# Attention scores in a two-layer decoder: from plain fp32 products to split single-pass products over 128 rows

## The chip, the cores and the metric

The kernel runs on one core of a Trainium2 chip. The metric is the time of one execution on the device, in microseconds (us); for the kernel before it is the median of three runs. Five engines work beside each other, each with its own queue in strict order: TensorE (PE in the profile, its weight loads PEld), VectorE (DVE), ScalarE (ACT), GpSimd (POOL) and SyncE (SP), which here issues DMAs. An instruction starts when those ahead of it on its engine have gone and when the semaphores that it waits for allow.

## The reference

256 tokens, 2048 features, two layers. The first is a retention layer, the second multi-head latent attention (MLA) with 16 heads; a squared-ReLU MLP follows each. All is fp32. The change touches the scores of the second layer: each head has a part of 128 features without position (`nope`) and a rotary part of 64 (`pe`), and the keys' rotary part is the same for all heads.

```python
q = (c_q @ w_uq).reshape(b, s, H, MLA_NOPE_DIM + MLA_ROPE_DIM)
q_nope = rms_norm(q[..., :MLA_NOPE_DIM], q_nope_norm)
q_pe = apply_rope(rms_norm(q[..., MLA_NOPE_DIM:], q_pe_norm), cos[:, :, None], sin[:, :, None])
...
sc = jnp.einsum('bhqd,bkhd->bhqk', qn, k_nope) + jnp.einsum('bhqr,bkr->bhqk', qp, k_pe)
sc = sc.astype(jnp.float32) * scale
sc = jnp.where(kpos[None, :] <= qpos[:, None], sc, -jnp.inf)
p = jax.nn.softmax(sc, axis=-1).astype(v.dtype)
return jnp.einsum('bhqk,bkhd->bqhd', p, v)
```

## The kernel before

**Split products.** A large product is made of parts: a matrix is split into `h`, rounded to a type with a short mantissa that PE takes in one pass (fp32r), and `l`, what is left. `split` (L131 to L137) writes `h` on ACT and `l` on DVE. PE then adds up three products, h by h, h by l and l by h (L192 to L194). Weights come by DMA into `raw` and are split half by half into `wh` and `wl`, each with five buffers. The small products of attention are plain fp32, which the profile counts as two passes each.

**Stages of the second layer.** Shared latent and rotary key (`kd`, `downed`), query latent (`dq`), keys and values (`ku`, `keyed`), queries and attention (`uq`), output projection (`wo`). Keys, queries and attention go in 8 blocks of two heads. The 256 tokens are two tiles of 128 (t = 0, 1).

**One block of attention.** `query` is called when the block's product is complete: ACT copies it from PSUM with its token scale (`qs`, L697). DVE squares it (`qu`), sums the squares of both parts, POOL makes the reciprocal roots (`qn_r`, `qp_r`), DVE multiplies by them (L705, L708) and rotates the `pe` part in four steps (L582 to L585). This is one norm chain for each token tile. Three pieces of weight product later PE transposes both parts (`qntp`, `qptp`), ACT copies them to SBUF (`qt`, `qpe`), and one piece later `score` (L739, L740) makes the products; a `pe` product has 64 rows, a `nope` product 128. DVE adds the mask (`p`, L745), takes maxima; ACT makes the exponentials; DVE divides. Two pieces later PE transposes `p` (`ptp`), ACT copies (`pt`), and `values` makes the products with the values (`ao`), which are split into `ot` for the output projection.

**What sets the order.** The code issues a block's steps some pieces of the weight product later (`later`, `tick`). A scheduler then orders each engine's queue by its own estimate of when operands and buffers are ready, so that an edit in one place moves rows of others. Tiles with one tag share a fixed number of buffers: `f2k` (14, among them `qs`, `qu`, `qt`, `qpe`, `p`, `pt`), `act` (20), PSUM `acc` (4), `tp` (2, for all transposes and for `ao`).

Of the kernel before, what the change touches and what calls it, by code (L numbers as in the profile page):

```python
# [49 lines left out]
def yoco(ctx: ExitStack, tc: tile.TileContext, a):  # L50
# [21 lines left out]
    def act_tile(name, dtype=F32R):  # L72
        """Two blocks of 128 features, each with its two halves (of precision, as a rule) side by side."""
        return pool.tile([P, 2, 2, S], dtype, tag="act", bufs=20, name=name)

    # Work that waits for other engines is issued some pieces of a product later.
    queue = []
# [18 lines left out]

# [1 line left out]
    gains = pool.tile([P, G_ALL], F32, name="gains")  # L98
# [15 lines left out]

# [1 line left out]
    def rstd(total, n, w, name):  # L116
        """(total / n + eps) ** -0.5 for [P, w] sums of squares."""
        m = small(w, f"{name}_m")
        nc.gpsimd.tensor_scalar(m, total, 1.0 / n, EPS, op0=ALU.mult, op1=ALU.add)
        r = small(w, f"{name}_r")  # L120
        nc.gpsimd.tensor_tensor(r, m, neg_half[:, :w], op=ALU.pow)
        return r
# [5 lines left out]
    def split(h, l, src, scale=None):  # L128
        """h + l = src * scale, each of 12 bits."""
        if scale is None:  # L130
            nc.scalar.copy(h, src)  # L131
            nc.vector.tensor_tensor(l, src, h.bitcast(F32), op=ALU.subtract)  # L132
        else:
            nc.scalar.activation(h, src, AF.Copy, scale=scale)  # L134
            nc.vector.scalar_tensor_tensor(
                l, src, scale, h.bitcast(F32), op0=ALU.mult, op1=ALU.subtract
            )  # L137
# [8 lines left out]
    def transposed(srcs, name):  # L146
        """[tokens, 128] pairs of both token tiles -> [128, 2, S] in PSUM."""
        tp = bank("tp", [2, S], name)
        for j in range(2):
            for t in range(NT):  # L150
                nc.tensor.transpose(tp[:, j, t * P : (t + 1) * P], srcs(t, j), ident)
        return tp

    def stream(w, chunk, cols, name, use, done=None, before=None):
        """use(half, parts of the weights) for both halves of a chunk of the weights."""
        raw = pool.tile([P, 2048], F32, tag="raw", bufs=3, name=f"{name}_raw")
        if before is None:
            nc.sync.dma_start(raw[:, :cols], w[chunk])
        n = cols // 2
        for half in range(2):  # L160
            wh = pool.tile([P, 1024], F32R, tag="wh", bufs=5, name=f"{name}_wh{half}")
            wl = pool.tile([P, 1024], F32R, tag="wl", bufs=5, name=f"{name}_wl{half}")
            cuts = 1
            if before is not None:
                cuts = 1 if half else 2
                m = n // cuts
                for i in range(cuts):
                    lo = half * n + i * m
                    nc.sync.dma_start(raw[:, lo : lo + m], w[chunk][:, lo : lo + m])
                    if i == 0:  # L170
                        before(half)
            m = n // cuts
            for i in range(cuts):
                lo = half * n + i * m
                split(wh[:, i * m : (i + 1) * m], wl[:, i * m : (i + 1) * m], raw[:, lo : lo + m])
# [132 lines left out]

# [81 lines left out]

# [33 lines left out]
    def ret_rope(acc, out, name, wait):  # L424
        """One head's rotated q or k by feature: [128, dk half, S]."""
        u = f2k([2, S], f"{name}_u")
# [110 lines left out]

# [1 line left out]
    def mlp(layer, act, row, done):  # L539
# [34 lines left out]

# [1 line left out]
    def pe_rope(dst, u, src, t, i, heads):  # L576
        """dst = the rotation of src [P, heads, ROPE], gains in the tables."""

# [10 lines left out]
    rc, ckv = [], []  # L589
    kpe_t = pool.tile([P, S], F32, name="kpe_t")  # L590

    def downed(acc, b):
# [8 lines left out]
        for t in range(NT):  # L601
# [9 lines left out]
            pe_rope(kp[:, 0, 0:1], kp[:, 1, 0:1], kp[:, 1, 1:2], t, 0, 1)  # L611
            nc.vector.tensor_copy(kp[:, 0, 1], kp[:, 0, 0])
            kps.append(kp)

        def turn():
            tp = bank("tp", [S], "kpe_tp")
            for t in range(NT):
                nc.tensor.transpose(tp[:, t * P : (t + 1) * P], kps[t][:, 0].rearrange("p h c -> p (h c)"), ident)
            nc.scalar.copy(kpe_t, tp)
# [10 lines left out]

# [1 line left out]
    ssq = [small(3, f"ssq{t}") for t in range(NT)]  # L632
# [25 lines left out]

# [1 line left out]
    k_t, v_s = [], []  # L660

    def keyed(acc, b):
        kv = act_tile(f"kv{b}", F32)
        kt, vt = kv[:, 0], kv[:, 1].rearrange("p t (h c) -> p t h c", h=2)
        v_s.append(vt)
# [13 lines left out]
        def turn():  # L679
            tp = transposed(lambda t, j: kr[t][:, 1, j], f"kntp{b}")  # L680
            nc.scalar.activation(kt, tp, AF.Copy, scale=gain(G_KN))
            k_t.append(kt)
# [5 lines left out]

# [1 line left out]
    nc.vector.tensor_scalar(gqn, gain(G_QN), scale, None, op0=ALU.mult)  # L690
    o_act = []

    def query(acc, b):
        qr = []
        for t in range(NT):
# [18 lines left out]
            pe_rope(pe.rearrange("p (h c) -> p h c", h=2), tmp, q[:, :, NOPE:], t, 1, 2)  # L714
            qr.append((q, pe))

        def turn():
            tp = transposed(lambda t, j: qr[t][0][:, j, 0:NOPE], f"qntp{b}")
            qt = f2k([2, S], f"qt{b}")
            nc.scalar.activation(qt, tp, AF.Copy, scale=gqn)  # L720
            tp = bank("tp", [S], f"qptp{b}")
            for t in range(NT):
                nc.tensor.transpose(tp[:, t * P : (t + 1) * P], qr[t][1], ident)
            qpe = f2k([S], f"qpe{b}")
            nc.scalar.copy(qpe, tp)
# [3 lines left out]

    def score(b, qt, qpe):  # L730
        """Scores [query, head, keys of tile 0 for both query tiles, then tile 1], then softmax."""
        sc = two_banks(f"s{b}")
        for hh in range(2):
            rows = slice(hh * ROPE, (hh + 1) * ROPE)
            for t in range(NT):
                dst = sc[:, hh, t * P : t * P + (t + 1) * P]
                qs = slice(t * P, (t + 1) * P)
                n = (t + 1) * P
                nc.tensor.matmul(dst, qt[:, hh, qs], k_t[b][:, hh, :n], start=True, stop=False)  # L739
                nc.tensor.matmul(dst, qpe[rows, qs], kpe_t[rows, :n], start=False, stop=True)  # L740
        p = [f2k([2, (t + 1) * P], f"p{b}{t}") for t in range(NT)]
# [138 lines left out]
```

## Time and profile before

| | us |
|---|---|
| Median of 3 runs (lowest, highest) | 2568.24 (2568.08, 2568.37) |
| Span of the profiled execution | 2566.0 |
| PE busy | 2554.7 |
| DVE busy | 1475.5 |
| ACT busy | 1233.7 |
| POOL busy | 135.7 |

The profiled execution's own time is not recorded apart from its span; the span is 2.2 us under the median. A row of a timeline gives the start in us from the span's start, the duration, engine, line, operation, output and inputs with shapes, a count of merged operations (x2) and, in brackets, the idle time of the engine before it and what ended it. Matmuls overlap, so the cost of one is the distance to the next start, not its duration.

### The profile page before, as it was taken

The page shows a single profiled execution, that of the slowest core. Times are in us where ns is not written, and L with a number is a line of the kernel's source. Part 1 is how long each engine was busy: PE and PEld are TensorE (multiplying, and loading weights), DVE is VectorE, ACT ScalarE, POOL GpSimd, SP SyncE. Part 2 cuts the span into 40 slices and gives each one's busy share as a digit, 9 for nine tenths or more (in the row PEclk, how much of TensorE's full clock was granted, in tenths as well). Part 3 has the DMA queues.
Part 4 walks back from the last instruction along what each step waited for, and adds up shares of the span by engine and source line. Part 5 has one row for each costly group of instructions (what it writes and reads, how often), then busy time and mean ns, then how long its engine had stood idle before and what let it go on. Part 6 is the DMA issues. An engine that isn't in the chain of part 4 may idle for free.

```text
span 2566.0 us, 31690 instructions
## 1 busy us (share of the span) xinstructions
PE 2554.7 (100%) x12786; PEld 2168.1 (84%) x12786; DVE 1475.5 (58%) x1828; ACT 1233.7 (48%) x1651; POOL 135.7 (5%) x211
## 2 busy tenths in 40 slices
PE   8999999999999999999999999999999999999999
PEld 7888888888888888888888888998888888888887
DVE  6655555554556644654565656776666446645654
ACT  6444444443445533543454566554555435534542
POOL 6200000000000000000000002221000000000000
PEclk9999999999999999999999999999999999999999
DMA  8555555555555555555555464444455555555554
GB/s 297 182 177 180 181 181 183 182 184 186 190 183 192 183 197 194 184 188 191 196 182 196 148 221 152 148 144 148 174 188 182 196 197 181 191 190 193 184 202 140
DMA packets 71571, 473.85 MB, mean 185 GB/s; under 512 B 8192, under 2 KB 9344, under 8 KB 18176
## 3 DMA queue, kind: packets, MB, share of 16 engines
q1 hardware_dynamic: 71280, 471.78, 52.1%
q8 instruction: 100, 1.64, 0.2%
q14 instruction: 47, 0.39, 0.0%
q10 hardware_dynamic: 144, 0.05, 0.0%
HBM read 469.70 MB, written 2.10 MB: 184 GB/s over the span
## 4 chain that ended last, share of the span: by engine, by line
PE 97%; POOL 2%; DMA 0%; DVE 0%; issue 0%; SPq 0%; DVEq 0%
PE u_acc L220 19%; PE u_acc L216 9%; PE d_acc L192 9%; PE d_acc L194 9%; PE d_acc L193 9%; PE ro_acc L194 2%; PE ro_acc L193 2%; PE ro_acc L192 2%; PE rv_acc L192 2%; PE rv_acc L194 2%; PE rv_acc L193 2%; PE rk_acc L220 2%; PE rq_acc L220 2%; PE rg_acc L192 2%; PE rg_acc L194 2%; PE rg_acc L193 2%
## 5 line engine op out<-in xcount | busy, mean ns | idle before, releaser
L220 PE MATMUL u_acc<-n,u_wh 128*128 128x512 f32 x2048 | 718.1, 398 | 0.0
L216 PE MATMUL u_acc<-n,u_wl 128*128 128x256 f32 x2048 | 564.8, 281 | 0.0
L132 DVE TENSOR_TENSOR d_wl<-d_raw,d_wh 128x1024 fp32r<-128x1024 f32 x256 | 313.6, 1225 | 321.6 <-ACT d_wh L131 321.6
L220 PEld LDWEIGHTS u_acc<-n,u_wh 128*128 128x128 f32 x2048 | 381.0, 188 | 88.8
L132 DVE TENSOR_TENSOR u_wl<-u_raw,u_wh 128x1024 fp32r<-128x1024 f32 x256 | 313.3, 1224 | 241.1 <-ACT u_wh L131 241.1
L131 ACT CAST d_wh<-d_raw 128x1024 fp32r<-128x1024 f32 x256 | 269.8, 1054 | 374.0 <-PE d_acc L194 347.4
L192 PE MATMUL d_acc<-d_wh,hid 128*128 128x512 f32 x1024 | 398.6, 389 | 0.0
L194 PE MATMUL d_acc<-d_wh,hid 128*128 128x512 f32 x1024 | 398.4, 389 | 0.0
L193 PE MATMUL d_acc<-d_wl,hid 128*128 128x512 f32 x1024 | 398.4, 389 | 0.0
L131 ACT CAST u_wh<-u_raw 128x1024 fp32r<-128x1024 f32 x256 | 269.1, 1051 | 260.2 <-PE u_acc L220 210.2
L216 PEld LDWEIGHTS u_acc<-n,u_wl 128*128 128x128 f32 x2048 | 386.7, 189 | 5.6
L194 PEld LDWEIGHTS d_acc<-d_wh,hid 128*128 128x128 f32 x1024 | 192.3, 188 | 40.0
L193 PEld LDWEIGHTS d_acc<-d_wl,hid 128*128 128x128 f32 x1024 | 192.3, 188 | 39.8
L192 PEld LDWEIGHTS d_acc<-d_wh,hid 128*128 128x128 f32 x1024 | 192.3, 188 | 39.4
L132 DVE TENSOR_TENSOR ro_wl<-ro_raw,ro_wh 128x1024 fp32r<-128x1024 f32 x64 | 78.4, 1225 | 84.2 <-ACT ro_wh L131 84.2
L132 DVE TENSOR_TENSOR rg_wl<-rg_raw,rg_wh 128x1024 fp32r<-128x1024 f32 (+1 forms) x68 | 78.9, 1166 | 60.9 <-ACT rg_wh L131 60.9
L131 ACT CAST ro_wh<-ro_raw 128x1024 fp32r<-128x1024 f32 x64 | 67.4, 1053 | 94.6 <-PE ro_acc L194 86.5
L192 PE MATMUL rg_acc<-rg_wh,a 128*128 128x512 f32 x256 | 101.1, 396 | 5.7 <-ACT a L134 5.7
L132 DVE TENSOR_TENSOR rv_wl<-rv_raw,rv_wh 128x1024 fp32r<-128x1024 f32 x64 | 79.3, 1250 | 41.3 <-ACT rv_wh L131 41.3
L131 ACT CAST rg_wh<-rg_raw 128x1024 fp32r<-128x1024 f32 (+1 forms) x68 | 67.8, 998 | 72.9 <-PE rv_acc L194 46.7
L193 PE MATMUL rg_acc<-rg_wl,a 128*128 128x512 f32 x256 | 100.3, 392 | 0.2 <-DVE rg_wl L132 0.2
L192 PE MATMUL rv_acc<-rv_wh,a 128*128 128x512 f32 x256 | 100.4, 392 | 0.0
(260 smaller groups left out, 4072.5 us busy)
## 6 DMA issues: line engine op xcount, KB each, us to landing
u_raw<-in_mlp_w SPq DMA_DIRECT2D x128, 1024.0 KB, 4.8
d_raw<-in_mlp_w SPq DMA_DIRECT2D x128, 1024.0 KB, 4.8
rv_raw<-in_ret_w_gv SPq DMA_DIRECT2D x32, 1024.0 KB, 4.7
ro_raw<-in_ret_w_out SPq DMA_DIRECT2D x32, 1024.0 KB, 4.7
rg_raw<-in_ret_w_gv SPq DMA_DIRECT2D x28, 1024.0 KB, 4.7
uq_raw<-in_mla_w_uq SPq DMA_DIRECT2D x24, 768.0 KB, 4.3
rq_raw<-in_ret_w_qk SPq DMA_DIRECT2D x16, 1024.0 KB, 4.8
rk_raw<-in_ret_w_qk SPq DMA_DIRECT2D x16, 1024.0 KB, 4.7
```

The lines of the kernel that those rows point to most:

```text
L131: nc.scalar.copy(h, src)
L132: nc.vector.tensor_tensor(l, src, h.bitcast(F32), op=ALU.subtract)
L192: nc.tensor.matmul(acc[t], ah, rh, start=k == 0, stop=False)
L193: nc.tensor.matmul(acc[t], ah, rl, start=False, stop=False)
L194: nc.tensor.matmul(acc[t], al, rh, start=False, stop=k == nk - 1)
L216: nc.tensor.matmul(acc[f][:, 0:S], wl[:, cols], a[:, 0], start=False, stop=False)
L220: nc.tensor.matmul(acc[f], wh[:, cols], a.rearrange("p i s -> p (i s)"), start=k == 0, stop=k == nk - 1)
```

## The change

Queries and keys of the scores are split into h and l, as weights are, and the score becomes five single-pass products for each head and token tile: three for the 128 `nope` features, and two for the rotary part. For these the 64 rotary features of a query's h and l are stacked to 128 rows (`qpp`, transposed into `qpe`). The rotary key is stored twice: once with its h in both halves, once with its l in the upper and zeros in the lower half (`parts` in `downed`), so that two products give (h + l) by h and h by l. `kt` and the values `v` become separate tiles of the `act` pool. `qt` is now two tiles, and for each token tile a `qpp` is added, all from `f2k`. Comments and docstrings were removed as well.

```diff
-    kpe_t = pool.tile([P, S], F32, name="kpe_t")
+    kpe_t = pool.tile([P, 2, S], F32R, name="kpe_t")
...
-            nc.vector.tensor_copy(kp[:, 0, 1], kp[:, 0, 0])
-            kps.append(kp)
+            parts = f2k([2, 2, ROPE], f"kpp{t}", F32R)
+            for i in range(2):
+                nc.scalar.copy(parts[:, 0, i], kp[:, 0, 0])
+            nc.vector.tensor_tensor(parts[:, 1, 0], kp[:, 0, 0], parts[:, 0, 0].bitcast(F32), op=ALU.subtract)
+            nc.vector.memset(parts[:, 1, 1].bitcast(F32), 0.0)
+            kps.append(parts.bitcast(F32))
...
-            for t in range(NT):
-                nc.tensor.transpose(tp[:, t * P : (t + 1) * P], kps[t][:, 0].rearrange("p h c -> p (h c)"), ident)
+            tp = transposed(lambda t, j: kps[t][:, j].rearrange("p h c -> p (h c)"), "kpe_tp")
...
-            nc.scalar.activation(kt, tp, AF.Copy, scale=gain(G_KN))
+            kt = act_tile(f"kt{b}")
+            split(kt[:, 0], kt[:, 1], tp, gain(G_KN))
...
-            qr.append((q, pe))
+            parts = f2k([2, 2, ROPE], f"qpp{b}{t}", F32R)
+            pe = pe.rearrange("p (h c) -> p h c", h=2)
+            split(parts[:, :, 0], parts[:, :, 1], pe)
+            qr.append((q, parts.bitcast(F32)))
...
-            qt = f2k([2, S], f"qt{b}")
-            nc.scalar.activation(qt, tp, AF.Copy, scale=gqn)
-            tp = bank("tp", [S], f"qptp{b}")
-            for t in range(NT):
-                nc.tensor.transpose(tp[:, t * P : (t + 1) * P], qr[t][1], ident)
-            qpe = f2k([S], f"qpe{b}")
+            qt = [f2k([2, S], f"qt{b}{i}", F32R) for i in range(2)]
+            split(qt[0], qt[1], tp, gqn)
+            tp = transposed(lambda t, j: qr[t][1][:, j].rearrange("p i c -> p (i c)"), f"qptp{b}")
+            qpe = f2k([2, S], f"qpe{b}", F32R)
             nc.scalar.copy(qpe, tp)
...
-                nc.tensor.matmul(dst, qt[:, hh, qs], k_t[b][:, hh, :n], start=True, stop=False)
-                nc.tensor.matmul(dst, qpe[rows, qs], kpe_t[rows, :n], start=False, stop=True)
+                qh, ql = (i[:, hh, qs] for i in qt)
+                kh, kl = (k_t[b][:, i, hh, :n] for i in range(2))
+                nc.tensor.matmul(dst, qh, kh, start=True, stop=False)
+                nc.tensor.matmul(dst, qh, kl, start=False, stop=False)
+                nc.tensor.matmul(dst, ql, kh, start=False, stop=False)
+
+                for i in range(2):
+                    nc.tensor.matmul(dst, qpe[:, hh, qs], kpe_t[:, i, :n], start=False, stop=i == 1)
```

The queues move with it. The first place is ACT between two scores, where the queries of block 4 are copied out of PSUM (`qs`, tile 0 and tile 1) and the transposed queries of block 3 to SBUF (`qt`, `qpe`). Lines are those of each kernel. Before:

```order
L131 CAST uq_wh_13690<-uq_raw 128x768
L697 ACTIVATE qs_13535<-uq_acc_13396,cq_r 128x384
L131 CAST uq_wh_13708<-uq_raw 128x768
L697 ACTIVATE qs_13556<-uq_acc_13397,cq_r 128x384
L720 ACTIVATE qt_13582<-qntp_13577,gqn 128x512
L725 COPY qpe_13587<-qptp_13584 128x256
L131 CAST uq_wh_13724<-uq_raw 128x768
L770 COPY pt_13593<-ptp_13589 128x384
```

In the changed kernel (`qpp_13650` and `qpp_13674` are the rotary parts of block 4, tile 0 and tile 1; `qs_13653` is its tile 1; its tile 0 was copied earlier, behind the `pt` of the score before):

```order
L131 CAST uq_wh_13952<-uq_raw 128x768
L131 CAST qpp_13650<-qu_13631 128x2x64
L701 ACTIVATE qs_13653<-uq_acc_13479,cq_r 128x384
L131 CAST uq_wh_14017<-uq_raw 128x768
L131 CAST uq_wh_14033<-uq_raw 128x768
L131 CAST qpp_13674<-qu_13655 128x2x64
L134 ACTIVATE qt_13682<-qntp_13677,gqn 128x512
L131 CAST uq_wh_14051<-uq_raw 128x768
L730 CAST qpe_13691<-qptp_13686 128x512
L780 COPY pt_13697<-ptp_13693 128x384
```

The second tile's `qs` has moved behind the first tile's `qpp`, and `qt` of block 3 behind the second tile's `qpp` of block 4.

The second place is DVE at the same point: the norm chains of the two tiles. Before:

```order
L705 TENSOR_TENSOR qs_13535<-qs_13535,qn_r 128x2x128
L708 TENSOR_TENSOR qs_13535<-qs_13535,qp_r 128x2x64
L699 TENSOR_TENSOR qu_13558<-qs_13556 128x384
L582 TENSOR_TENSOR qu_13537<-qs_13535,petab_82 128x128
L583 TENSOR_TENSOR qu_13537<-qs_13535,petab_82 128x2x32
L584 TENSOR_TENSOR qu_13537<-qs_13535,petab_82 128x2x32
L701 TENSOR_REDUCE sq_13560<-qu_13558 128x2
L585 TENSOR_TENSOR qu_13537<-qu_13537 128x128
L702 TENSOR_REDUCE sq_13560<-qu_13558 128x2
L705 TENSOR_TENSOR qs_13556<-qs_13556,qn_r 128x2x128
```

In the changed kernel, from the end of the first tile's chain:

```order
L585 TENSOR_TENSOR qu_13631<-qu_13631 128x128
L132 TENSOR_TENSOR uq_wl_13953<-uq_raw,uq_wh_13952 128x768
L132 TENSOR_TENSOR qpp_13650<-qu_13631,qpp_13650 128x2x64
L703 TENSOR_TENSOR qu_13655<-qs_13653 128x384
L705 TENSOR_REDUCE sq_13657<-qu_13655 128x2
L706 TENSOR_REDUCE sq_13657<-qu_13655 128x2
L132 TENSOR_TENSOR uq_wl_14018<-uq_raw,uq_wh_14017 128x768
L709 TENSOR_TENSOR qs_13653<-qs_13653,qn_r 128x2x128
...
L585 TENSOR_TENSOR qu_13655<-qu_13655 128x128
L132 TENSOR_TENSOR qpp_13674<-qu_13655,qpp_13674 128x2x64
L135 SCALAR_TENSOR_TENSOR qt_13683<-qntp_13677,gqn,qt_13682 128x512
```

The two chains were interleaved and now stand one after the other; behind them stands the low part of `qt`.

The third place is PE at the score of block 3. Before:

```order
L194 MATMUL uq_acc_13602<-uq_wh_13621,cq_11856 128x384
L739 MATMUL s_13637<-kv_12388,qt_13582 128x128
L740 MATMUL s_13637<-kpe_t,qpe_13587 128x128
L739 MATMUL s_13637<-kv_12388,qt_13582 128x256
L740 MATMUL s_13637<-kpe_t,qpe_13587 128x256
```

In the changed kernel:

```order
L745 MATMUL s_13741<-kt_12559,qt_13682 128x128
L746 MATMUL s_13741<-kt_12559,qt_13682 128x128
L192 MATMUL uq_acc_13932<-uq_wh_13936,cq_11856 128x384
L193 MATMUL uq_acc_13932<-uq_wl_13937,cq_11856 128x384
L778 MATMUL ptp_13693<-cst,p_13535 128x128
L778 MATMUL ptp_13693<-cst,p_13536 128x128 x2
L778 MATMUL ptp_13699<-cst,p_13535 128x128
L778 MATMUL ptp_13699<-cst,p_13536 128x128 x2
L747 MATMUL s_13741<-kt_12559,qt_13683 128x128
L750 MATMUL s_13741<-kpe_t,qpe_13691 128x128 x2
```

The score's first two products now stand before two of uq and the transposes of `p` of the block before, the other eighteen behind them.

More of the change, by code (lines that the diff above doesn't have):

```diff
@@ L611, in downed @@
             pe_rope(kp[:, 0, 0:1], kp[:, 1, 0:1], kp[:, 1, 1:2], t, 0, 1)
-            nc.vector.tensor_copy(kp[:, 0, 1], kp[:, 0, 0])
-            kps.append(kp)
+            parts = f2k([2, 2, ROPE], f"kpp{t}", F32R)
[4 more added lines that the diff above has]
+            kps.append(parts.bitcast(F32))
         def turn():
-            tp = bank("tp", [S], "kpe_tp")
-            for t in range(NT):
-                nc.tensor.transpose(tp[:, t * P : (t + 1) * P], kps[t][:, 0].rearrange("p h c -> p (h c)"), ident)
+            tp = transposed(lambda t, j: kps[t][:, j].rearrange("p h c -> p (h c)"), "kpe_tp")
             nc.scalar.copy(kpe_t, tp)
@@ L657, in yoco @@
         gemm(a["mla_w_dq"], b * 4, act_q, KD, 512, f"dq{b}", lambda acc, b=b: queried(acc, b))
-    k_t, v_s = [], []
+    k_t, v_s, vs = [], [], []
     def keyed(acc, b):
-        kv = act_tile(f"kv{b}", F32)
-        kt, vt = kv[:, 0], kv[:, 1].rearrange("p t (h c) -> p t h c", h=2)
+        if b % 2 == 0:
+            vs.append(act_tile(f"v{b}", F32))
+        vt = vs[-1][:, b % 2].rearrange("p t (h c) -> p t h c", h=2)
         v_s.append(vt)
@@ L733, in score @@
         for hh in range(2):
-            rows = slice(hh * ROPE, (hh + 1) * ROPE)
             for t in range(NT):
```

## The prediction

> **What bounds the kernel now.** I read the page first, then the waits of TensorE (PE), then timelines of the query stage, where the change lies. The first rows are from the page, the last from the waits of PE.
>
> ```profile
> span 2566.0 us, 31690 instructions
> PE 2554.7 (100%) x12786; PEld 2168.1 (84%) x12786; DVE 1475.5 (58%) x1828; ACT 1233.7 (48%) x1651; POOL 135.7 (5%) x211
> PE rg_acc L192 <- ACT a L134: 5.7, 1, 5.7
> ```
>
> PE is busy for the whole span but for 5.7 us at the start. What is taken from PE shortens the kernel, and any wait put into its queue lengthens it, one for one. The span stands to the median of the runs, 2568.24 us, as 2566.0 and 2.2 us around it; I carry the 2.2.
>
> One turn of the query stage, from score to score, in the table of stretches (columns: length, then busy time of PE, PEld, DVE, ACT, POOL):
>
> ```profile
> 1673.62:1692.95 19.33, 19.33 (x109) 17.35 (x109) 14.89 (x38) 9.97 (x21) 4.82 (x8) 1.00 0.38 130
> ```
>
> PE fills its 19.33 us. DVE is busy for 14.9 of them: little room before it, too, is a bound. PE's own rows of that turn, and two of the key stage for a price:
>
> ```profile
> 1687.43 0.60 PE L151 MATMUL qntp<-cst,qs 128*128 128x128 f32 x4
> 1687.87 0.38 PE L723 MATMUL qptp<-cst,qu 128*128 128x128 f32 x2
> ...
> 1692.96 0.38 PE L739 MATMUL s<-kv,qt 128*128 128x128 f32 x2
> 1693.28 0.48 PE L740 MATMUL s<-kpe_t,qpe 64*128 64x128 f32 x2
> 1693.69 0.70 PE L739 MATMUL s<-kv,qt 128*128 128x256 f32 x2
> ...
> 1697.04 0.70 PE L779 MATMUL ao<-pt,kv 128*128 128x256 f32 x2
> ...
> 1698.37 0.42 PE L192 MATMUL uq_acc<-uq_wh,cq 128*128 128x384 f32 x1
> 1698.62 0.34 PE L193 MATMUL uq_acc<-uq_wl,cq 128*128 128x384 f32 x1
> 1698.80 0.34 PE L194 MATMUL uq_acc<-uq_wh,cq 128*128 128x384 f32 x1
> ```
> ```profile
> 1484.10 0.28 PE L194 MATMUL kd_acc<-kd_wh,n 128*128 128x256 f32 x1
> 1484.22 0.28 PE L192 MATMUL kd_acc<-kd_wh,n 128*128 128x256 f32 x1
> ```
>
> Durations overlap, so prices are distances between starts. A score costs 1697.04 - 1692.96 = 4.08 us: each plain product is two passes (x2). A split product (fp32r) is one pass; at 256 columns they follow each other every 0.12 us. Transposes follow every 0.44 / 4 = 0.11 us, and a uq product takes 0.18 us.
>
> **What PE gains.** Per score, 8 plain products (4.08 us) become 20 single passes, ten of 256 columns and ten of 128. For 256 columns I take 0.12 us. A split product of 128 columns stands nowhere in this trace: its lower bound is the transposes' 0.11 us, its upper one the 0.41 us / 2 = 0.21 us of a pass in the row at 1693.28. I take 0.11, since it has the same shape as the transposes and one pass; hence 20 x 0.115 = 2.3 us. Eight scores save 8 x (4.08 - 2.3) = 14.2 us. Against it stand two more transposes per score and two for the rotary key, 18 x 0.11 = 2.0 us. Net, PE has 12.2 us less to do, and a turn would be 19.33 - 4.08 + 2.3 + 0.22 = 17.8 us if nothing made PE wait.
>
> **What the others gain, and where it lies.** The key splits add one DVE operation for each of 8 head pairs (0.6 us, by the `ot` row below, of the same size). In the new order each stands ahead of a multiply that waits for POOL:
>
> ```profile
> 1588.23 0.43 DVE L676 TENSOR_TENSOR kn<-kn,kn_r 128x256 f32<-128x256 f32 x1 [1.09 <-POOL kn_r L121]
> ```
>
> It fits into that 1.09 us, so I cost it at nothing; without that cover it is 8 x 0.6 = 4.8 us of DVE time, which the six weight splits in a row after the stage partly take up.
>
> The query splits are another matter, because of their place. The new order puts, on ACT, the copies of the rotary parts (`qpp`) of block b+1 ahead of `qt` of block b, and `qs` of the second token tile behind the first tile's `qpp`. Each `qpp` waits for DVE's whole norm and rotation of its tile. So PE's score b waits for `qt`, that for two norms one after the other, and these begin only after score b-1: a loop, which the old order does not have (there nothing on ACT ahead of `qt` waits for DVE). I go round it with prices from one turn of the old trace, on DVE, ACT and POOL:
>
> ```profile
> 1680.32 1.01 DVE L745 TENSOR_TENSOR p<-s,cst 128x256 f32<-128x256 f32 x2
> 1681.76 0.40 ACT L755 ACTIVATE p<-p,mx 128x128 f32<-128x128 f32 x1 [1.86 <-DVE mx L750]
> 1682.17 0.68 DVE L132 TENSOR_TENSOR ot<-ao,ot 128x512 fp32r<-128x512 f32 x1
> 1683.53 1.56 ACT L131 CAST uq_wh<-uq_raw 128x768 fp32r<-128x768 f32 x2
> 1683.87 1.01 DVE L761 TENSOR_SCALAR p<-p,inv 128x128 f32<-128x128 f32 x4
> 1684.79 2.69 DVE L132 TENSOR_TENSOR uq_wl<-uq_raw,uq_wh 128x768 fp32r<-128x768 f32 x3
> ...
> 1687.72 0.56 DVE L699 TENSOR_TENSOR qu<-qs 128x384 f32<-128x384 f32 x1 [0.24 <-ACT qs L697]
> 1688.32 0.42 DVE L701 TENSOR_REDUCE sq<-qu 128x2 f32<-128x256 f32 x1
> 1688.42 0.58 ACT L697 ACTIVATE qs<-uq_acc,cq_r 128x384 f32<-128x384 f32 x1
> 1688.83 1.02 POOL L119 TENSOR_SCALAR qn_m<-sq 128x2 f32<-128x2 f32 x1 [11.28 <-DVE sq L701]
> 1688.85 0.95 DVE L132 TENSOR_TENSOR uq_wl<-uq_raw,uq_wh 128x768 fp32r<-128x768 f32 x1
> 1688.89 0.68 ACT L720 ACTIVATE qt<-qntp,gqn 128x512 f32<-128x512 f32 x1
> 1689.46 0.37 ACT L725 COPY qpe<-qptp 128x256 f32<-128x256 f32 x1
> 1690.65 0.42 DVE L705 TENSOR_TENSOR qs<-qs,qn_r 128x256 f32<-128x256 f32 x1 [0.86 <-POOL qn_r L121]
> 1691.94 0.29 DVE L708 TENSOR_TENSOR qs<-qs,qp_r 128x128 f32<-128x128 f32 x1 [0.86 <-POOL qp_r L121]
> 1692.62 0.28 DVE L582 TENSOR_TENSOR qu<-qs,petab 128x128 f32<-128x128 f32 x1
> 1693.09 0.41 DVE L701 TENSOR_REDUCE sq<-qu 128x2 f32<-128x256 f32 x1
> 1693.42 0.28 DVE L585 TENSOR_TENSOR qu<-qu 128x128 f32<-128x128 f32 x1
> 1693.59 0.19 POOL L119 TENSOR_SCALAR qn_m<-sq 128x2 f32<-128x2 f32 x1 [1.68 <-DVE sq L701]
> ```
>
> From the mask of score b-1 (`p`, time 0):
> - The value product runs on PE for 1698.37 - 1697.04 = 1.3 us; ACT copies `ot` (0.6, as DVE's `ot`), then the four exponentials, 1683.53 - 1681.76 = 1.8: 3.7. The reciprocal (0.3 to the scaling row), the first sum of squares (0.33, from 1693.09 to 1693.42), the scaling (0.92) and the second sum (0.2): 5.5.
> - First tile: its multiply by `qn_r` comes at once at 5.5, or 0.7 later if POOL could not work beside the scaling. To the multiply by `qp_r` 1.29, itself 0.2, a weight split 0.87, three rotation steps 0.47, another split 0.87, the last step 0.2: 9.4 to 10.1.
> - ACT: `qpp` 0.3 (half the columns of `qpe`), `qs` 0.5; meanwhile DVE does a split and the low part of `qpp`, 1.1: 10.5 to 11.2.
> - Second tile: 0.60 to its sum, 2.33 on to the multiply, 1.29, 0.2, 0.47, 0.87, 0.2: 16.5 to 17.2.
> - ACT: `qpp` and `qt`, 0.3 + 0.6: 17.4 to 18.1. Here PE can begin score b.
> - After two products and two of uq, PE stands before the transposes of `p` until `qt`'s low part and `qpe` free their banks: a weight cast 0.75 and `qpe` at 512 columns 0.57, so 1.3 us after `qt`; three of six transposes 0.35; the other 18 products 2.1; 0.3 until DVE sees them: 21.5 to 22.2.
>
> So a turn takes 21.5 to 22.2 us where PE has 17.8 us of work: it stands still for 3.7 to 4.4 us, 4.1 in the middle. The rows speak for both ends: at 1688.83 POOL's first step took 1.02 us beside a weight split, at 1693.59 only 0.19 beside a reduction; for a scaling beside it there is no row, hence the middle. [...]
>
> Four turns are of this kind (scores 1 to 5): 16.4 us. The next ends with output projections, 60 products of 0.23 us (rows below) instead of 72 of 0.18, 0.8 us more work for PE: a wait of 3.3. Before scores 0 and 1 the same two norms stand ahead of `qt`: for score 0, by the same steps, 0.5 + 5.1 + 0.8 + 6.0 + 0.9 = 13.3 us from the first `qs` on, against 54 uq products and 8 transposes, 10.6 us: 2.7; for score 1 I take the same, an estimate. Score 7 has no norms ahead of it. The waits sum to 16.4 + 3.3 + 5.4 = 25.1 us. **Sum:** 25.1 - 12.2 = 12.9 us more; 2566.0 + 12.9 + 2.2 = 2581 us. With the loop's two ends, and the three other waits at 2 to 4 us each, 2577 to 2586.
>
> **Rivals.** *The narrow product or the clock costs more* (slower still). At 0.21 us for 128 columns PE gains 8 us less and the loop grows as PE's work does, so the waits stay: 2589. Nearly the same would follow if the waits slowed the array:
>
> ```profile
> 5.73 0.80 PE L192 MATMUL rg_acc<-rg_wh,a 128*128 128x512 f32 x1 [5.73 <-ACT a L134]
> 6.32 0.63 PE L193 MATMUL rg_acc<-rg_wl,a 128*128 128x512 f32 x1
> 6.75 0.63 PE L194 MATMUL rg_acc<-rg_wh,a 128*128 128x512 f32 x1
> ...
> 10.02 0.39 PE L193 MATMUL rg_acc<-rg_wl,a 128*128 128x512 f32 x1
> 10.25 0.40 PE L194 MATMUL rg_acc<-rg_wh,a 128*128 128x512 f32 x1
> ```
>
> After 5.7 us of idleness products came every 0.43 us instead of 0.23 for 4 us, a loss of 1.9 us; seven such losses at 1 us each, as part falls into waiting, give 2588. Against it: my waits are about 4 us, not 5.7. [...]
>
> *No new wait* (faster, the other side): if DVE comes through both norms by the time PE gets to the score, the 12.2 us show: 2556. This decides itself where the way to `qt`, 17.4 us in my working, falls under the 14 us that PE needs to come round to the score. For it: ACT is busy only 10 of 19 us, and PE has no wait at all in this stage now. Against: DVE is held by POOL 0.86 us twice per tile, and the order leaves it nothing to overlap.
>
> *Half of it*: the way to `qt` is 2 us shorter than I find; the waits are then about 12 us and cancel the gain: 2568, no change.
>
> **How the numbers follow.** The loop as worked out: 0.52, 2581 us. The dearer product: 0.12, 2589; the clock: 0.08, 2588. Cancelled: 0.13. No new wait: 0.15. Within 0.2% (5 us), about what a measurement here tells from no change, lies the cancelled case: faster 0.15, same 0.13, slower 0.72. The range takes in the cancelled case and the dearer ones and leaves out most of the faster: 2562 to 2592; the likeliest case has 2577 to 2586.
>
> **What would show it.** Right: PE waits of 3 to 4 us for ACT `qt` before six or seven scores, a turn of about 22 us, DVE with no long wait but for POOL and for `p`, score products spread at 0.11 to 0.12 us, half of the score's PE time gone. Wrong: PE without idle time in the query stage (the order's wait is hidden); 128-column products at 0.2 us; products after a wait at double distance (the clock); idle PE in the key stage, where I see none.

## The result, and the profile after

The changed kernel takes 2598.5 us (median of four runs, 2593.32 to 2599.53) against 2568.16 us of the kernel before, measured beside it: a ratio of 1.0114, 95% interval 1.0100 to 1.0128, some 30 us slower. Forecast were 2581 us and a range to 2592: the sign was right, the size was not. The profiled run is the fastest of the four, 2593.32 us with a span of 2591.5 us.

From the page of the changed kernel, and from the waits of PE (time in all, times, longest):

```profile
span 2591.5 us, 31842 instructions
PE 2556.7 (99%) x12836; PEld 2179.4 (84%) x12836; DVE 1490.8 (58%) x1862; ACT 1240.1 (48%) x1671; POOL 140.6 (5%) x211
PE s L745 <- ACT qt L134: 21.8, 7, 3.7
PE rg_acc L192 <- ACT a L134: 5.7, 1, 5.7
PE qptp L151 <- DVE qpp L132: 2.0, 1, 2.0
```

PE waits for `qt` before seven of the eight scores, as forecast. These waits, with the one at the first `qptp`, which was not foreseen, make 23.8 us where 25.1 were forecast. But PE is also busy for 2.0 us *more* than before, though it has less to do. The stretches from score to score tell why. The columns are length, then busy time of PE, PEld, DVE, ACT and POOL, the clock granted to PE, DMA share and GB/s:

```profile
1675.96:1698.74 22.78, 19.67 (x115) 18.88 (x115) 15.14 (x38) 10.63 (x24) 4.97 (x8) 0.93 0.31 105
1698.74:1721.78 23.04, 19.87 (x115) 18.88 (x115) 15.14 (x38) 10.64 (x24) 4.96 (x8) 0.93 0.29 102
1721.78:1743.21 21.43, 18.29 (x114) 17.29 (x114) 15.14 (x38) 10.53 (x24) 4.97 (x8) 1.00 0.39 128
1743.21:1767.24 24.03, 20.91 (x117) 19.49 (x118) 16.87 (x37) 12.54 (x25) 5.24 (x8) 0.93 0.37 133
```

The third turn has the full clock: 21.43 us with 3.14 us of idleness. The first two have the same work and nearly the same waits (3.1 and 3.2 us), but a clock of 0.93, and are 1.4 and 1.6 us longer. (The fourth has other work too: it ends with products of the output projection.) How the clock fell is seen in steps of 3.41 us round the wait before 1675.96, and round the one before 1721.78 (same columns):

```profile
1672.76:1676.17 3.41, 0.21 (x2) 0.21 (x2) 2.45 (x8) 1.15 (x3) 0.23 (x1) 1.00 0.09 32
1676.17:1679.58 3.41, 3.41 (x16) 3.28 (x16) 1.45 (x2) 2.38 (x5) 0.00 (x0) 0.50 0.52 203
1679.58:1682.99 3.41, 3.41 (x27) 3.30 (x27) 1.81 (x4) 0.51 (x2) 0.00 (x0) 1.00 0.00 0
1717.13:1720.54 3.41, 1.51 (x9) 1.19 (x7) 2.14 (x7) 0.00 (x0) 1.46 (x3) 1.00 0.21 85
1720.54:1723.95 3.41, 2.14 (x16) 1.79 (x17) 2.18 (x5) 2.83 (x6) 0.00 (x0) 1.00 0.57 216
```

The stretch with 3.20 us of idleness is followed by exactly one at half clock, while PE works without a pause; the one with 1.90 us is followed by the full clock. Seven stretches at half clock stand in the query stage: two in a row after the wait before the first score, none after the waits before the fourth (1721.78) and the seventh, and one after each of the others. Summed over steps of 0.1 us, PE's busy time times what is missing of the clock, they cost 11.8 us. From PE's timeline, the first of five split products of 128 columns and the first of 256 behind them, at half clock and at the full clock:

```profile
1652.37 0.31 PE L745 MATMUL s<-kt,qt 128*128 128x128 f32 x1
...
1653.33 0.52 PE L745 MATMUL s<-kt,qt 128*128 128x256 f32 x1
...
1724.30 0.22 PE L745 MATMUL s<-kt,qt 128*128 128x128 f32 x1
...
1724.81 0.33 PE L745 MATMUL s<-kt,qt 128*128 128x256 f32 x1
```

The five take 0.96 us in the first case and 0.51 us in the second: 0.10 us each at the full clock.

So the account of the profiled run is: idle time 23.5 us more than before (2591.5 - 2556.7, less 2566.0 - 2554.7), 11.8 us of work lost to half clock, and 9.8 us saved by the products. The last is what the other two leave of the 25.5 us between the spans; it is not measured by itself.

### The profile page after: what moved, and what is told of

Its sections match the earlier page's. It is cut to its first block, busy times and chain, and to the rows that moved or that the text cites. A ratio compares the mean times of both kernels' runs of the same rounds, so it can differ in the third digit from the quotient of the medians.

```text
span 2591.5 us, 31842 instructions
## 1 busy us (share of the span) xinstructions
PE 2556.7 (99%) x12836; PEld 2179.4 (84%) x12836; DVE 1490.8 (58%) x1862; ACT 1240.1 (48%) x1671; POOL 140.6 (5%) x211
```

## The experiments

One table first; medians are of the runs of each, each ratio is to the kernel before on the same chip, and the last three columns are made from the profiled run as above, in us more than before: idle time of PE, work lost to half clock, work saved (what the other two leave).

| Kernel | Median | Ratio, 95% interval | Idle | Lost | Saved |
|---|---|---|---|---|---|
| the change | 2598.5 | 1.0114, 1.0100 to 1.0128 | 23.5 | 11.8 | 9.8 |
| 1: qpp in own buffers | 2601.06 | 1.0129, 1.0112 to 1.0146 | 26.5 | 18.0 | 11.4 |
| 2: other work ahead of each score | 2620.29 | 1.0205, 1.0190 to 1.0220 | 25.5 | 16.8 | 12.4 (with 22 us more work) |
| 3: 16 shared buffers | 2595.4 | 1.0109, 1.0093 to 1.0124 | 24.0 | 11.7 | 10.2 |
| 4: plain fp32, zeros to 128 rows | 2558.68 | 0.9964, 0.9951 to 0.9977 | 2.1 | 0 | 11.6 |
| 5: rotary half, own buffers | 2561.73 | 0.9977, 0.9967 to 0.9986 | 4.0 | 1.7 | 11.4 |
| 6: rotary half, shared buffers | 2591.51 | 1.0093, 1.0078 to 1.0108 | 22.2 | 13.4 | 11.0 |
| 7: nope half | 2632.53 | 1.0251, 1.0236 to 1.0266 | 27.5 | 40.3 | 2.6 |
| 8: change, `qt` ahead of the norms | 2567.13 | 0.9996, 0.9987 to 1.0006 | 8.5 | 2.9 | 11.6 |
| 9: change, low part by POOL | 2570.59 | 1.0009, 1.0000 to 1.0018 | 11.3 | 1.7 | 10.2 |
| 10: the change again | 2597.43 | 1.0109, 1.0092 to 1.0126 | 25.4 | 16.6 | 11.7 |

### 1. The buffers of qpp

```diff
-            parts = f2k([2, 2, ROPE], f"qpp{b}{t}", F32R)
+            parts = pool.tile([P, 2, 2, ROPE], F32R, tag="qpp", bufs=4, name=f"qpp{b}{t}")
```

> One line differs from the changed kernel: the split rotary parts (qpp) get four buffers of their own instead of two of the 14 shared f2k buffers. The order of ACT then has both qs copies and qt ahead of the two qpp copies, and the two norm chains interleave again. Theory A (the waits of PE for qt come from that order, and the order from the shared buffers; the rest of the loss is PE at half speed after those waits): no PE wait for qt, granted clock 1.000 or 0.999, PE busy about 2545 us (2554.7 of before less the 9.9 that the changed kernel saves once its seven half-speed stretches of 1.7 us are taken off), median 2556 to 2561 us. Rival B (the wait is inherent in two norms by DVE between two scores, whatever the buffers): waits of 3 us stay before most scores, 2585 us or more. Rival C (the products themselves got slower, by mixing kinds): no waits, but PE busy stays near 2557 and the median near 2566 to 2570.

Theory A fell. The wait for `qt` on ACT is gone, and others as long stand elsewhere. Waits of PE, and from DVE's timeline the norm multiplies of the second tile and the low part of `qt`:

```profile
PE ptp L778 <- DVE qt L135: 10.6, 6, 2.4
PE ptp L778 <- ACT qpe L730: 9.8, 6, 1.8
PE s L747 <- DVE qt L135: 5.6, 1, 5.6
```
```profile
1687.27 0.43 DVE L709 TENSOR_TENSOR qs<-qs,qn_r 128x256 f32<-128x256 f32 x1 [0.69 <-POOL qn_r L121]
1687.61 0.28 DVE L132 TENSOR_TENSOR qpp<-qu,qpp 128x128 fp32r<-128x128 f32 x1
1688.55 0.29 DVE L712 TENSOR_TENSOR qs<-qs,qp_r 128x128 f32<-128x128 f32 x1 [0.66 <-POOL qp_r L121]
1688.76 0.74 DVE L135 SCALAR_TENSOR_TENSOR qt<-qntp,gqn,qt 128x512 fp32r<-128x512 f32 x1
```

The transposes of `p` need the two PSUM banks that `qntp` and `qptp` hold. Before, one ACT copy each freed them. Now `qntp` is read by DVE too, and that low part stands behind the multiplies of the next block's norms; `qpe` stands behind the first `qpp` on ACT. PE stops at `ptp` instead of at the score, but for the first score. Rival B names about the right length of wait (3.5 us per turn, in two pieces), but that two norms between two scores are too long "whatever the buffers" is refuted by runs 5 and 8. Rival C, without waits, falls as well.

### 2. Other work in the waits

```diff
         sc = two_banks(f"s{b}")
+        for i in range(12):
+            v = cq[i % 6].rearrange("p j i s -> p j (i s)")
+            nc.tensor.matmul(sc[:, i % 2], cq[0][:, 0, 0, 0:P], v[:, 0], start=True, stop=True)
```

> The changed kernel with twelve products of 512 columns (about 0.23 us each, 2.7 us) ahead of each score, written to the score's own bank and overwritten by it: PE has work in most of the time in which it waited, the order of ACT and DVE round the loop stays (qt behind both qpp). Theory A: the loop still sets a turn of about 21.4 us, as in the one turn of the changed kernel that ran at full speed, but PE idles about 1 us per turn and no longer falls to half speed there; granted clock 0.999 or more, median 2578 to 2585 us, so faster than the changed kernel although PE has 22 us more work. Rival D (the half speed costs little, since it falls into waiting; the loop itself is longer than worked out): no gain, 2593 to 2600 us; if the waits were not there to be filled, 22 us more than the changed kernel, about 2620.

This did not test what it should. The scheduler put the score earlier in PE's queue, in most turns 45 products behind the transposes of the queries instead of 64, twelve of them the added ones, so the added work took the place of other work and the waits stayed. Waits of PE:

```profile
PE s L748 <- ACT qt L134: 22.9, 7, 3.7
PE qptp L151 <- DVE qpp L132: 2.0, 1, 2.0
```

It is slower than the change by about the 22 us that the 96 products take at 0.23 us, as the last case of its expectation has it. What idle time costs without half clock is therefore not shown by this run.

### 3. Two more shared buffers

```diff
-        return pool.tile([P, *shape], dtype, tag="f2k", bufs=14, name=name)
+        return pool.tile([P, *shape], dtype, tag="f2k", bufs=16, name=name)
```

> The changed kernel with 16 shared f2k buffers instead of 14, as many more as a block's qpp tiles take. In its order qt still stands behind both qpp on ACT, and qs of the second tile behind the first qpp, since the buffer that this qs takes over is freed only by the transposes of the block before. Theory A (the order decides, not the number of buffers): waits of PE for qt of about 3 us stay, clock 0.992 to 0.996, 2588 to 2600 us. Rival E (two buffers were short, two more cure it): 2556 to 2561 us as with buffers of their own.

As theory A says: idle and lost time stay within 0.5 us of the change's. The order, which this edit leaves as it is, decides, not a shortage of two buffers.

### 4. Plain fp32 with 128 rows

```diff
-    kpe_t = pool.tile([P, S], F32, name="kpe_t")
+    kpe_t = pool.tile([P, 2, S], F32, name="kpe_t")
+    nc.gpsimd.memset(kpe_t, 0.0)
...
-            nc.scalar.copy(kpe_t, tp)
+            for i in range(2):
+                rows = slice(i * ROPE, (i + 1) * ROPE)
+                nc.scalar.copy(kpe_t[rows, i], tp[rows])
...
-                nc.tensor.matmul(dst, qpe[rows, qs], kpe_t[rows, :n], start=False, stop=True)
+                nc.tensor.matmul(dst, qpe[:, qs], kpe_t[:, hh, :n], start=False, stop=True)
```

> The kernel before, all in plain fp32 and without any split of queries or keys; only the rotary key is stored twice, for each head of a pair with zeros in the other head's 64 rows, so that the rotary products have 128 rows like the others. The same 64 features are summed, the other rows add zeros. Before, products of 128 and of 64 rows alternate in a score and stand 0.41 us (128 columns) and 0.63 us (256 columns) apart, while plain products of 128 rows among themselves (ao) stand 0.22 and 0.44 us apart. If the alternation costs the 0.19 us, a score falls from 4.08 to 4 x 0.22 + 4 x 0.44 = 2.64 us, eight scores save 11.5 us, and nothing else changes: 2556 to 2558 us, clock 1.000, no waits. If instead the 64-row product is simply dear by its columns, or the passes are what costs, the score stays near 4 us and the time within 2 us of before.

2558.68 us, 0.7 us above the expected range; PE has two waits for `qt`, 1.8 us in all, that were not expected. The first products of a score and the first of `ao` behind it, on PE:

```profile
1689.81 0.38 PE L741 MATMUL s<-kv,qt 128*128 128x128 f32 x2
1690.03 0.39 PE L742 MATMUL s<-kpe_t,qpe 128*128 128x128 f32 x2
1690.25 0.60 PE L741 MATMUL s<-kv,qt 128*128 128x256 f32 x2
1690.69 0.59 PE L742 MATMUL s<-kpe_t,qpe 128*128 128x256 f32 x2
...
1692.43 0.59 PE L781 MATMUL ao<-pt,kv 128*128 128x256 f32 x2
```

A score takes 2.62 us instead of 4.08, in the same number of passes: what was dear was not the passes but the 64-row products among 128-row ones. In the kernel before, the 128-row products of a score are as dear as the 64-row ones (0.63 us from 1693.69 to 1694.32, as from there to 1694.95, instead of 0.44), which speaks for the alternation; no run has 64-row products alone. PE before, behind the rows of the prediction:

```profile
1694.32 0.70 PE L740 MATMUL s<-kpe_t,qpe 64*128 64x256 f32 x2
1694.95 0.49 PE L739 MATMUL s<-kv,qt 128*128 128x128 f32 x2
```

The change's own score, 2.29 us at the full clock (run 8), is only 0.33 us shorter and needs two more transposes, so most of what it saves on PE has this source. This version beats both kernels, by 0.4% and 1.5%.

### 5 and 6. The rotary half alone, with own and with shared buffers

`qt` and the keys without position are plain fp32 as before, the rotary part is split and stacked as in the change. Run 5 has the edit of run 1 besides; run 6 does not. Cut:

```diff
-            qt = [f2k([2, S], f"qt{b}{i}", F32R) for i in range(2)]
-            split(qt[0], qt[1], tp, gqn)
+            qt = f2k([2, S], f"qt{b}")
+            nc.scalar.activation(qt, tp, AF.Copy, scale=gqn)
```

> Only the rotary half of the change: rotary queries and keys split and stacked to 128 rows, the 128 features without position in plain fp32 as before (qt is one ACT copy, no low part by DVE), and the qpp tiles in four buffers of their own. In its order qt and qpe stand ahead of both qpp on ACT, and nothing that frees a bank of transposes stands behind a norm chain. Theory F (PE waits where a bank of transposes or qt is given free only behind the next block's norms: on ACT because qpp stands ahead of qt, on DVE because the low part of qt stands behind the norms; half speed follows each wait): no wait in the queries, clock 1.000, a score of 4 x 0.22 + 4 x 0.44 / 2 for the plain products, that is 1.3 us, and 0.9 for eight single passes, 2.2 us instead of 4.08, less 0.2 for two more transposes: 8 x 1.65 = 13 us saved, median 2554 to 2558 us. Rival B (two norms between two scores are too long whatever the queues): waits of 3 us, 2585 us or more.

> The same as the run beside it (only the rotary half of the change), but with qpp in the shared f2k buffers, as in the change: twelve tiles of a block share 14. In its order qs of the second tile stands behind the first qpp on ACT and qt behind both. Theory F: the ACT half of the loop alone is enough: PE waits for qt of about 3 us before six or seven scores, about 22 us in all, half speed after most of them, median 2585 to 2597 us, though the computation is that of the run beside it. Rival G (only the low part of qt on DVE makes the waits): 2554 to 2558 us as the run beside it.

Same computation, same engines, 29.8 us apart by where four small tiles lie. Waits of PE, first of run 5, then of run 6:

```profile
PE ptp L773 <- ACT qt L726: 1.9, 1, 1.9
PE ao L784 <- ACT pt L775: 1.6, 5, 0.4
```
```profile
PE ptp L773 <- ACT qt L726: 16.7, 6, 3.8
PE s L742 <- ACT qt L726: 4.9, 1, 4.9
```

The ACT half of the loop is shown: with `qpp` ahead of `qt` the waits are there without any low part of `qt`; with `qt` ahead they are gone, and both norms still lie between two scores. Run 5 is 3.7 us above its expected range: one wait of 1.9 us remains, which brought one half-clock stretch (1.7 us), `ao` waits for `pt` (1.6 us), and 11.4 us instead of 13 were saved.

### 7. The other half alone

Queries and keys without position are split; the rotary part stays plain with 64 rows; there is no `qpp`.

> Only the other half of the change: queries and keys without position split (three single passes instead of a plain product), the rotary part in plain fp32 with 64 rows as before, no qpp. In its order the ACT copies stand as in the kernel before, qt ahead of everything that waits for DVE; the low part of qt on DVE stands behind the second tile's multiplies. Theory F: the DVE half of the loop alone is enough: PE waits at the transposes of p for the bank that the low part of qt still holds, about 3 us per turn and 15 to 24 us in all, none for ACT qt or qpe; PE saves only about 5 us, since 64-row products stay; with half speed 2580 to 2600 us. Rival H (only qpp on ACT makes the waits): no waits, 2561 to 2566 us.

The DVE half of the loop is shown as well: ACT's `qt` and `qpe` are waited for nowhere, though the waits, 28.3 us, are longer than the 15 to 24 expected. Waits of PE, then the stretch behind the first of them:

```profile
PE ptp L775 <- DVE qt L135: 22.7, 6, 3.9
PE s L744 <- DVE qt L135: 5.6, 1, 5.6
```
```profile
1639.39:1653.04 13.65, 11.03 (x31) 8.60 (x32) 5.73 (x13) 2.63 (x8) 1.41 (x3) 0.50 0.17 59
```

The time is beyond the range, since half clock lasted 10.2 or 13.7 us behind each of the seven waits, not 3.4: this row is four windows of 3.41 us, and in the second and third PE was busy throughout, mostly with the score's short and alternating products, without getting the full clock back. 40.3 us were lost. Why these windows did not bring it back is open.

### 8. The split of qt ahead of the norms

```diff
-        later(3, turn)
+        queue.append((clock[0] + 3, -2, turn))
```

with the edit of run 1; `turn` is what transposes and splits the queries.

> The whole change with qpp in buffers of its own and the transposes and split of qt issued ahead of the next block's norms: in its order the high part of qt (ACT) and the low part (DVE) stand ahead of both norm chains, which interleave. Theory F: no wait for qt behind norms; what remains is DVE itself, 15.1 us busy per turn and about 4.2 us in which it waits for POOL's roots and for the exponentials, so a turn of 19.3 to 20.1 us where PE has 17.7: waits of 1.6 to 2.4 us per turn, few half-speed stretches, median 2563 to 2578 us. Rival B (two norms between two scores): 2590 us or more, as with own buffers alone. Rival I (DVE's waits are covered by other work, as in the kernel before): 2556 to 2559 us.

Within the range: 31.4 us less than the change with the same products, by the order and the place of four small tiles, and no different from the kernel before. Waits of PE:

```profile
PE ptp L778 <- ACT qpe L730: 4.4, 2, 4.2
PE ptp L778 <- DVE qt L135: 3.7, 5, 1.1
```

From the second turn on, the waits are 0.7 to 1.1 us, and no stretch at half clock follows; the only two follow the wait of 4.2 us at the first score. DVE's waits are covered better than worked out: a turn takes 18.6 us.

### 9. The low part by POOL

```diff
-            split(qt[0], qt[1], tp, gqn)
+            qf = pool.tile([P, 2, S], F32, tag="qf", bufs=1, name=f"qf{b}")
+            nc.scalar.activation(qf, tp, AF.Copy, scale=gqn)
+            nc.scalar.copy(qt[0], qf)
+            nc.gpsimd.tensor_tensor(qt[1], qf, qt[0].bitcast(F32), op=ALU.subtract)
```

> The whole change, same products, with both halves of the loop undone: qpp in four buffers of its own, and the bank of the transposed queries is emptied by one ACT copy (qf, one buffer of its own), from which ACT takes the high part and POOL, not DVE, the low part (34 instead of 40 small buffers make room). In its order qf and qpe stand ahead of both qpp on ACT, and the low part on POOL behind the roots of the next block's first tile only. Theory F (the waits come from the two places, not from the work): no wait for a bank; the low part ends about 5 us (roots) and 1 to 2.5 us (POOL's subtraction, of which no row exists) after the block's product, PE wants it after 6 us, so 0 to 1.5 us per turn; no window of 3.41 us is more than half idle but perhaps at the first score; 2557 to 2568 us, 30 to 40 us less than the change. Rival B (two norms between two scores): 2585 us or more. Rival J (POOL's subtraction holds the second tile's roots up, and DVE with them): a turn of 20 us, 2570 to 2580 us.

The long waits are gone, and 27 us with them (run 10 is the change on the same chip), but the time is 2.6 us above the expected range and inside rival J's: a turn takes 19.4 us. J's mechanism is half right. The second tile's roots are not held up, but while POOL subtracts, which takes 1.27 us (1 to 2.5 expected, without a row for it), DVE's multiply by `qp_r` takes 1.35 us; for the second tile, with POOL at rest, it takes 0.29. From the timelines of POOL and DVE, and the waits of PE:

```profile
1678.52 1.27 POOL L730 TENSOR_TENSOR qt<-qf,qt 128x512 fp32r<-128x512 f32 x1
1678.59 1.35 DVE L712 TENSOR_TENSOR qs<-qs,qp_r 128x128 f32<-128x128 f32 x1 [0.86 <-POOL qp_r L121]
...
1683.58 0.29 DVE L712 TENSOR_TENSOR qs<-qs,qp_r 128x128 f32<-128x128 f32 x1 [0.85 <-POOL qp_r L121]
```
```profile
PE ptp L781 <- ACT qf L728: 5.9, 6, 1.6
PE s L750 <- POOL qt L730: 5.0, 6, 2.3
```

### 10. The change again

> The changed kernel once more, unaltered, for another profile and more times. In the eight profiles so far the clock is granted in windows of 3.41 us on a fixed grid: every window at full speed in which PE idled 0.55 of the time or more was followed by one at half speed, none with 0.54 or less. If that holds, this run shows about 24 us of idle time again, as the order is the same, but the waits lie otherwise to the grid, so that the work lost to half speed may be another: 12 to 19 us, and the span 2591 to 2598 us goes with it. If the times spread for another reason, the idle time differs and the lost work stays 12.

Idle time 25.4 us, lost work 16.6 us, span 2596.3 us: 4.8 us longer than the first profile, with 4.8 us more lost to half clock and 1.9 us more idle time (its first wait is 4.9 us instead of 3.3); 1.9 us more were saved, of which about 1 is the slow start of the kernel (last section), which ended at 8.9 instead of 10.5 us. The four runs of the change show the same: granted clocks of 0.995, 0.993, 0.992 and 0.992 with spans of 2591.5, 2596.4, 2597.8 and 2597.0 us. By these clocks the spread of the change's times is that of its half-clock stretches, and the median run lost some 5 us more than the first profile shows, an estimate from the two profiles. To the expectation's "every window" there is one exception, in the first profile: the one at 1717.13, idle for 1.90 of 3.41 us (0.56), was followed by the full clock. In run 10 five waits brought two half-clock stretches each and one brought one, eleven instead of seven. A turn behind a wait of 3.1 us shows what that costs:

```profile
1699.05:1723.08 24.03, 20.91 (x115) 20.16 (x115) 15.16 (x38) 10.63 (x24) 4.97 (x8) 0.86 0.29 98
```

With the same work and the same idle time (3.1 us), such a turn takes 21.4 us without a half-clock stretch, 22.8 to 23.0 with one (both in the first profile) and 24.0 with two.

## Why the prediction was right and wrong

**What bounds the kernel, and the path round the loop: right.** The legs from the mask of one score to `qt`, which the prediction worked out from the old trace, stand in the new one within its bounds. DVE, POOL and ACT of the change:

```profile
1704.21 1.02 DVE L755 TENSOR_TENSOR p<-s,cst 128x256 f32<-128x256 f32 x2 [3.81 <-PE s L750]
...
1708.30 1.00 DVE L771 TENSOR_SCALAR p<-p,inv 128x128 f32<-128x128 f32 x4
...
1709.62 0.43 DVE L709 TENSOR_TENSOR qs<-qs,qn_r 128x256 f32<-128x256 f32 x1
```
```profile
1708.47 0.19 POOL L119 TENSOR_SCALAR qn_m<-sq 128x2 f32<-128x2 f32 x1 [12.75 <-DVE sq L705]
1708.75 0.84 POOL L121 TENSOR_TENSOR qn_r<-qn_m,neg_half 128x2 f32<-128x2 f32 x1
```
```profile
1713.64 0.30 ACT L131 CAST qpp<-qu 128x128 fp32r<-128x128 f32 x1 [1.40 <-DVE qu L585]
...
1720.84 0.30 ACT L131 CAST qpp<-qu 128x128 fp32r<-128x128 f32 x1 [4.39 <-DVE qu L585]
1721.05 0.68 ACT L134 ACTIVATE qt<-qntp,gqn 128x512 fp32r<-128x512 f32 x1
```

First `qpp` at 9.4 us (9.4 to 10.1 forecast), second at 16.6 (16.5 to 17.2), PE's score 17.6 us after the mask (17.4 to 18.1), and a turn at full clock of 21.43 us, just under the 21.5 to 22.2. The lower end holds, since POOL worked beside the scaling (L771): the multiply by `qn_r` came 5.4 us after the mask, with a wait of only 0.1 us. POOL's first step took 0.19 us there, and its second 0.84, where it took 0.69 for the second tile with DVE at rest: beside the scaling POOL was slower by at most 0.15 us, where the prediction allowed for 0.7. One reading is wrong: PE idled for 11.3 us of the old span (2566.0 - 2554.7), not 5.7; the rest are two waits near 58 us (1.1) and 4.2 us behind its last product. The sum does not suffer, since they are there after the change too.

**What PE gains: right within 2 us.** A score takes 2.29 us at the full clock (run 8; 2.3 forecast); 9.8 to 11.7 us were saved where 12.2 were forecast. The dearer narrow product fell: 0.10 us at full clock, and the 0.19 to 0.21 seen elsewhere are half clock. The size came from measured distances, so it does not hang on the reason; by run 4 the reason is the row counts more than the passes.

**Key splits at nothing: right.** PE waits for nothing in the key stage.

**The wait: its places right, its sum near by luck in part.** It stands before the seven scores named, none before the eighth. The four steady turns waited 3.1 us each where 3.7 to 4.4 were forecast, since the turn was at its lower end and PE was busy for 18.3 us of it, not 17.8; the wait before score 6 (the first is score 0, as in the prediction) was 2.3 us, not 3.3. Against these 5 us too little stand 1.6 us too much before scores 0 and 1 (3.3 and 3.7, not 2.7 each) and the unforeseen 2.0 us at the first `qptp`: 23.8 of 25.1 us in all.

**The cause of the wait: right for this kernel, but not the whole.** The prediction put it on ACT's queue alone, and took the low part of `qt` for 1.3 us behind it; in the changed kernel PE does wait for ACT's `qt`. Runs 1, 5, 6 and 7 show two loops, each enough by itself: ACT's, through `qpp`, and DVE's, through the bank that the low part holds. With `qt` ahead of `qpp` on ACT, but its low part still behind the norms on DVE (run 1), the kernel stays as slow.

**The clock: the step that failed.** The prediction gave it a chance of 0.08 and 1 us for each wait, "Against it: my waits are about 4 us, not 5.7." The 5.7 us were the only long wait in the old trace, and at its very start; they could not show that less isn't enough. A wait of 2.0 us was (before 1634.31 in the first profile, with half clock from 1635.21 on). The sum of 2581 us thus had nothing for the clock. Instead of seven times 1 us at small odds, the change lost 11.8 us in one profile and 16.6 in the other. With it, the sum closes, as it must, since what was saved is taken as the rest: 12.9 forecast, less 1.6 of idle time (25.1 to 23.5), plus 2.4 not saved, plus 11.8 is 25.5 us, the difference of the spans; the median run, with some 5 us more lost, comes near the 30 us measured. The loss does not "fall into waiting" as the price of 1 us assumed: it strikes the score itself, which lies on the loop, so the turns grow by it (22.8 to 23.0 us with one half-clock stretch and 24.0 with two, beside 21.4). That half clock is what made these turns longer rests on turns of the same kernel side by side (first profile and run 10); no run has all of the change's waits and the full clock throughout (run 2 was meant for that).

**The rival on the other side** (no new wait, 2556 us) decided itself where it said, by the way to `qt`; run 5 comes within 6 us of it with the loop undone. The rival with half of the wait fell in the same place: the way to `qt` was 17.6 us, not 2 us less than worked out.

## What to carry to other kernels

The split that let a second engine read a PSUM bank moved the bank's release into that engine's queue here (runs 1 and 7: the transposes of `p` waited 10.6 and 22.7 us for DVE's `qt`): look for what stands ahead of the reader there, and for what PE needs the bank for. When PE is the bound, price each new wait with the half clock that may follow it; here one of 2.0 us was followed by it, and the lost work was half of the idle time or more (11.8 us beside 23.5, and 16.6 beside 25.4 in run 10). And before splitting a plain product for its passes, look whether it alternates between row counts: filling up with zeros gave about the same gain on PE here (11.6 us in run 4, beside 9.8 and 11.7 of the change) for one more ACT copy and one fill with zeros in all.

## What the runs showed of the hardware

**The falls to half clock lie on a grid.** In the query stage of ten profiles all 48 falls to half clock begin on a grid of 3.41 us of their run (start times agree with it to 0.01 us). Of the windows of that grid at full clock, 49 have 1.87 us of idleness or more, and 48 of them are followed by half clock (the one that is not has 1.90 us); the 19 with 1.0 to 1.81 us are all followed by the full clock. The border lies near 0.54 of the window in these profiles, and the wait's whole length did not decide: in the first profile the wait of 3.1 us before 1721.78, which lay across two windows (1.90 and 1.27 us of idleness in them), cost nothing more, and the one of 2.0 us before 1634.31, within one window, cost a whole window at half clock.

**What the full clock came back after.** In the same stage, outside run 7, 40 of the 41 half-clock windows in which PE had no idle time were followed by the full clock, and 20 of the 21 with 0.23 us of idleness or more by another at half clock. So here a wait that lasted into a half-clock window mostly cost a second one, as in run 10. In run 7, 14 windows without idle time did not bring the full clock back, so idle time is not all that counts.

**Alternating row counts cost about 0.19 us a product here.** Plain products of 128 rows stand 0.22 us (128 columns) and 0.44 us (256) apart, those of a score that alternates 128 and 64 rows 0.41 and 0.63 us (run 4 and the kernel before).

**The slow start is not in the clock column.** The first products of the kernel stand at double distance until 10.0 us before and 10.5 us after, while the granted clock reads 1.00 there. The trace's own record of the clock begins only at 9.8 and 10.5 us: where it has nothing, the column shows the full clock.
